# Modulation products of layer 0 in pairs of row blocks, layer 1's partition sums in one piece

## The chip, the cores and the metric

One core of a Trainium2 chip runs the kernel. The metric is device microseconds of one execution, the median over several runs. A profiled execution of the same kernel, whose rows are shown below, has its own time.

## The reference, cut to what matters

A trunk of two layers works on 128 context tokens and 256 latent tokens of 1024 features. Each layer takes a conditioning vector (one for context, one for latent tokens), makes six modulation vectors of it with a 1024 x 6144 matrix, and uses them around a mixer and a feed-forward block:

```
def trunk_layer(x, cvec, lp, init, latent):
    mod = jax.nn.silu(cvec.astype(jnp.float32)) @ lp['w_mod'] + lp['b_mod']
    sh1, sc1, g1, sh2, sc2, g2 = jnp.split(mod[:, None, :], 6, axis=-1)
    h = rmsnorm(x, lp['norm_mix_pre']) * (1.0 + sc1) + sh1
    mix, states = mixer(h, lp, init, latent)      # retention | Hyena long convolution | mLSTM
    x1 = x + g1 * rmsnorm(mix, lp['norm_mix_post'])
    h = rmsnorm(x1, lp['norm_ffn_pre']) * (1.0 + sc2) + sh2
    out = x1 + g2 * rmsnorm(conv_ffn(h, lp), lp['norm_ffn_post'])
```

The change concerns the first line alone: the product of two vectors (context and latent) with `w_mod`, 25 MB a layer.

## The kernel before

The large projections (`w_in`, `w_out`, `w_up`, `w_down`) run on TensorE with weights split into a high and a low part: a raw chunk is loaded (`raw`, line 333, issued by SyncE, called SP), ScalarE casts it (`hi`, L278), VectorE subtracts (`lo`, L255), and three products are made for each block (activations `hh`, `hl` by weights `hi`, `lo`). Every matmul is recorded at line 208 (`mm`), every transpose at L212 (`tp`); `b` is a PSUM bank.

The modulation matrix of a layer is cut in three superblocks of 2048 columns (s = 0, 1, 2) and eight row blocks of 128 rows, 1 MB each (`mraw`, two buffers). A row block by the two conditioning columns (`sil`) is a narrow product: 4 products of 512 columns whose outputs lie at partitions 0, 32, 64 and 96 of one bank. These are the narrow products of this text; all others, which fill the array, are called wide. Superblock 0 of layer 0 is made at the start. Superblocks 1 and 2 of layer 0 (`mod`) are streamed beside the projections of the mixer: they are two generators in a queue, and `fill`, called once for each chunk of weights of the mixer's projections (`weights`), takes one step of it. A step loads one row block and issues its four products. After the eighth, `mod_finish` loads a bias tile (`modbm`, in a buffer of the same two), adds it on VectorE, writes gates to DRAM (`gd`), and transposes the result on TensorE.

For layer 1 (`mod_beside`) the products are made on VectorE during layer 0's feed-forward block: two accumulators `macc` (one for each conditioning vector, r = 0 and 1) of 2048 columns take each row block times one column of `sil`, in pieces of 512 columns. At the end eight products with `onesel` (a column of ones that picks one output row) sum over partitions on TensorE into one bank, for each of the three superblocks.

Each engine works its instructions off in order. That order comes from a list scheduler that goes by priorities and by its own estimate of times, except where the code fixes it (`issue_after`: behind a given instruction on its engine; `high_priority`: earlier in the list). SP issues the loads in its own order too, and a load whose buffer isn't free yet holds back those behind it.

Of the kernel before, what the change touches and what calls it, by code (L numbers as in the profile page):

```python
# [37 lines left out]
# the largest float32 by which half a turn stays within the range of the sine  # L38
# [3 lines left out]
# ---------------------------------------------------------------- host side: layout and shape constants  # L42
# [8 lines left out]
def _constants():  # L51
# [6 lines left out]
    # minus one for each of the three parts of a head's row  # L58
# [10 lines left out]
    # even and odd tokens, the lower half of the frequencies: the upper half is their sum with  # L69
    # the other sign, conjugated  # L70
# [31 lines left out]
def _layout(inp):  # L102
# [8 lines left out]
    # rows of the modulation vectors: block j of 512 columns sits at partitions 32j (context) and 32j + 1 (latent)  # L111
# [14 lines left out]
    def token_major(m):  # L126
        # (L, D, 4*384) -> per group of 384 columns, two chunks of four 128-row blocks
        m = m.reshape(L, 2, 4, 128, 4, 384)
        return m.transpose(0, 4, 1, 3, 2, 5).reshape(L, 8, 128, 1536)
# [3 lines left out]
    # the gates ride along with the first 384 columns  # L133
# [7 lines left out]
    # per-partition columns  # L141
# [11 lines left out]
    # the filter networks of both layers side by side, 64 partitions each  # L153
# [34 lines left out]
# ---------------------------------------------------------------- device side  # L188

class Trunk:  # L190
    # banks of the accumulators of w_out, by block of tokens
# [13 lines left out]
    # -------- small helpers  # L205
# [8 lines left out]
    def in_order(self, engine):  # L214
        """The engines in self.strict take their work as it is written here."""
        last = getattr(self, engine)
        return self.tc.issue_after(last.ins) if engine in self.strict and last else nullcontext()

    def after(self, *last):
        """Behind these on their engines."""  # L220
        stack = ExitStack()
        for i in last:
            stack.enter_context(self.tc.issue_after(i.ins))
        return stack

    # -------- PSUM: eight banks, each a queue of its own
# [3 lines left out]
    def turn(self, s):  # L230
        """The next bank of a set taken in turns."""
# [54 lines left out]
    def rms(self, s2):  # L286
        """The reciprocal root of the mean square, from the two halves of the mean."""
# [6 lines left out]
    def log_sigmoid(self, out, z, P, n):  # L294
        """min(z, 0) - log1p(exp(-|z|)), log1p with the rounding of its argument put back."""
# [11 lines left out]
    # -------- weights  # L307
# [18 lines left out]
    def load_weights(self):  # L326
        """The loads of the next chunk of the stream, in halves."""
# [14 lines left out]
    def splits(self, key, raws):  # L342
        """High and low parts of a chunk, in steps."""
        halves, steps = [], []
        # at the turn of a block the buffers are still taken, but the one of the spectra is idle
# [5 lines left out]
        for raw in raws:  # L351
            m = raw.shape[1]
            hi, lo = new("hi"), new("lo")
            # finer where the vector engine also has the norms between two projections to do
# [22 lines left out]
    # -------- setup  # L377
    def setup(self):
# [21 lines left out]
        # silu of both conditioning vectors, as stationary columns  # L400
# [15 lines left out]
    def start(self, fp):  # L416
        """Modulation and normalised rows of the first projection, and the filter spectra of both
        layers beside them; the loads in the order in which they are needed."""
# [7 lines left out]
        def rows(k):  # L426
            """Modulation weights, in the buffers of the weights as long as these are idle."""
# [44 lines left out]
        def warm(n):  # L472
            """Products of no use that take the tensor engine's clock out of its rest while the first
            loads are on their way."""
            for _ in range(n):
                self.mm(spin, idle[:, :128], idle)
# [16 lines left out]
        # the bias  # L493
# [69 lines left out]
    def fill(self, n=1):  # L563
        """Streams the next blocks of modulation weights beside the projections."""
# [11 lines left out]
    def mod(self, l, s):  # L576
        """Superblock s of the modulation of layer l: (sh1 | sc1), (g1 | sh2), (sc2 | g2)."""
        nc = self.nc
        ps = self.md()
        for k in range(KD):  # L580
            raw = self.wraw.tile([128, 2048], F32, tag="mraw", name=self.nm("mraw"), bufs=2)
            nc.sync.dma_start(raw, self.I["w_mod"][l, 128 * k:128 * k + 128, 2048 * s:2048 * s + 2048])
            for j in range(4):
                self.mm(ps[32 * j:32 * j + 32, :], self.sil[:, k, :], raw[:, 512 * j:512 * j + 512], k == 0, k == KD - 1)
            if k < KD - 1:
                yield False
        self.mod_finish(l, s, ps, self.md)

    def mod_beside(self, l, s):
        """The same with the products on the vector engine, where only that one has time to spare."""  # L590
# [18 lines left out]
        for j in range(4):  # L609
            for r in range(2):  # L610
                self.mm(ps[32 * j:32 * j + 32, :], self.onesel[:, r, :], acc[r][:, 512 * j:512 * j + 512], r == 0, r == 1)
# [33 lines left out]
    def gate_rows(self, l, g):  # L645
        """A gate times its norm gain, over all partitions: [128, context / latent, D]."""
# [5 lines left out]
    # -------- hyena filter spectra  # L652
    def filter_hidden(self, fp, w1, w2, col, meanwhile):
        """The hidden layers of the filter networks of both layers: [128, tokens] for each layer,
        64 rows of its own and a row of ones."""
# [4 lines left out]
        for i, wt in enumerate((w1, w2)):  # L660
# [5 lines left out]
            # in turns, less the nearest whole number  # L666
# [15 lines left out]
    def filter_taps(self, fp, l, h, w3):  # L682
        """Sum and difference of the forward and the backward filters."""
# [15 lines left out]
    def filter_spectra(self, fp, l, taps):  # L699
        nc = self.nc  # L700
        # spectra [frequency, tile, cos / sin, order, channel]
# [15 lines left out]
    def butterfly(self, s, d, a, b):  # L717
        """s = a + b, d = a - b, of two PSUM tiles."""
# [8 lines left out]
    # -------- normalised, modulated activations, transposed and split  # L727
# [4 lines left out]
    def norm_pre(self, t):  # L732
        """A diagonal of the reciprocal root mean squares of the rows of x."""
# [9 lines left out]
    def norm_T(self, t, where, h, psf):  # L743
        """Tokens of block t modulated, transposed and split into the tiles of h."""
# [31 lines left out]
    def norm_T_after(self, *a):  # L776
        """norm_T behind the products queued so far."""
# [6 lines left out]
    def group(self, key, l, g, between=None):  # L784
        """Token-major columns g of an input projection: three [128, 384] accumulators."""
# [12 lines left out]
        if key == "m" and g == 0:  # L798
            # the first tokens are there before the last ones
# [36 lines left out]
    def heads_T(self, src, tag):  # L836
        """[128 tokens, 4 * 96] -> [96, 4, 128]."""
# [7 lines left out]
    def head_norm(self, src, out):  # L845
        """out = src * 0.5 * rsqrt(mean(src^2) + eps) by head, [128, 4, 96]; src in SBUF."""
# [9 lines left out]
    # -------- gates of the mLSTM  # L856
    def gates(self, l, pss):
# [5 lines left out]
        # [token, direction, tile, head]  # L863
# [6 lines left out]
        # the splits of the next weights let the gates go first  # L870
# [3 lines left out]
    def stabilisers(self, l, g5, lf):  # L874
# [9 lines left out]
        # rows [head, direction, tile, token]  # L884
# [13 lines left out]
        # [head, (previous, last), direction, tile]  # L898
# [21 lines left out]
        # previous and last stabilisers over all partitions: [128, 2, direction, tile, head]  # L920
# [22 lines left out]
    def row_parts(self, mr):  # L943
        """The stabilisers as three bfloat16 parts that add up to them, 32 partitions apart."""
# [13 lines left out]
    # -------- mLSTM  # L958
# [117 lines left out]
    def channel_major(self, outs, ws, hh, hl):  # L1076
        """Two [128 columns, 384 tokens] products from a chunk [rows of k, 2 * 128 columns]."""
# [9 lines left out]
    # -------- Hyena  # L1087
    def long_conv(self, z, o):
        """z: two [128 channels, 384] tiles -> PSUM tiles of the long convolution, the latent rows
        with the even ones first."""  # L1090
# [473 lines left out]
```

## Time and profile before

| | |
|---|---|
| median of 3 runs | 1358.76 us (1355.83 to 1360.96) |
| span of the profiled execution | 1355.0 us |
| what lies between the median and that span | 3.8 us |
| TensorE busy in the span | 1339.3 us, 99% |
| VectorE busy | 890.6 us, 66% |
| ScalarE busy | 568.8 us, 42% |
| DMA moved | 217.27 MB, mean 160 GB/s |

The span runs from the first to the last instruction of the profiled execution, and sums are made against it. Ends of matmuls are modelled in the profile, so durations of neighbours overlap a little, and the distance of two starts is the safer measure of what an instruction costs. Layer 0's streamed modulation lies between 60 and 222 us of the span, layer 1's sums at 437, 539 and 645 us.

### The profile page before, as it was taken

To read this page: it belongs to the slowest core of one execution; us is meant where nothing else is said; L and a number is where in the kernel's file an instruction comes from. 1 tells how busy PE (TensorE), PEld (TensorE's weight loads), DVE (VectorE), ACT (ScalarE), POOL (GpSimd) and SP (SyncE) were. 2 spreads that over 40 slices of the span, in tenths; PEclk is the share of its full clock that TensorE was granted. 3 is DMA by queue.
4 is the path that set the end of the run, shared out by engine and by line. 5 is a ranking of instruction groups with operands and counts; after the bars stand their busy time and mean duration, and the time that the engine had idled before them with its cause. 6 is when DMAs were issued, how large, how long until landed. Compare 5 with 4: busy or idle time off the path is not lost.

```text
span 1355.0 us, 19419 instructions
## 1 busy us (share of the span) xinstructions
PE 1339.3 (99%) x7527; PEld 1206.1 (89%) x7527; DVE 890.6 (66%) x1594; ACT 568.8 (42%) x944; POOL 35.3 (3%) x64
## 2 busy tenths in 40 slices
PE   8999999999999999999999999999999999999997
PEld 2788788889998998899899999988999999999996
DVE  5657666667887899799557578666645545545445
ACT  3654253464333333333247543546433333333333
POOL 1100000000000000000000000000000000000000
PEclk9999999999999999999999999999999999999999
DMA  9864557344665565665335232424434334333331
GB/s 354 290 249 148 181 168 238 101 164 151 212 227 172 191 237 176 212 221 181 116 112 192 95 95 73 143 92 173 143 118 137 126 117 136 124 121 131 124 122 50
DMA packets 59101, 217.27 MB, mean 160 GB/s; under 512 B 7214, under 2 KB 9456, under 8 KB 53632
## 3 DMA queue, kind: packets, MB, share of 16 engines
q1 hardware_dynamic: 59008, 216.02, 46.7%
q8 instruction: 59, 0.97, 0.3%
q14 instruction: 34, 0.28, 0.1%
HBM read 210.06 MB, written 5.94 MB: 159 GB/s over the span
## 4 chain that ended last, share of the span: by engine, by line
PE 91%; DMA 5%; DVE 2%; ACT 1%; issue 1%; POOL 0%; SPq 0%; DVEq 0%; POOLq 0%; ACTq 0%
PE b L208 90%; DMA mraw<-in_w_mod 1%; DMA raw<-in_w_up 1%; PE b L212 1%; DMA hi<-in_w_mod 1%; DMA lo<-in_w_mod 1%; DMA raw<-in_w_in_m 1%; DVE lo L255 1%; ACT junk L274 0%; ACT hi L278 0%; DMA c_tri<-in_c_tri 0%; DMA w<-in_f_w 0%; DVE mr L908 0%; POOL rr L291 0%; DVE x L266 0%
## 5 line engine op out<-in xcount | busy, mean ns | idle before, releaser
L255 DVE TENSOR_TENSOR lo<-raw,hi 128x1024 fp32r<-128x1024 f32 (+3 forms) x288 | 321.2, 1129 | 216.9 <-ACT hi L278 214.3
L278 ACT CAST hi<-raw 128x1024 fp32r<-128x1024 f32 (+3 forms) x288 | 275.4, 973 | 411.7 <-PE b L208 387.5
L208 PE MATMUL b<-hh,lo 128*128 128x384 f32 (+1 forms) x1120 | 367.9, 336 | 0.0
L208 PE MATMUL b<-hh,hi 128*128 128x384 f32 (+2 forms) x1120 | 364.8, 334 | 0.0
L208 PE MATMUL b<-hl,hi 128*128 128x384 f32 x1088 | 362.5, 338 | 0.0
L208 PEld LDWEIGHTS b<-hh,hi 128*128 128x128 f32 x1120 | 205.7, 188 | 4.6 <-issue 2.5
L208 PEld LDWEIGHTS b<-hh,lo 128*128 128x128 f32 x1120 | 208.0, 188 | 0.1
L208 PEld LDWEIGHTS b<-hl,hi 128*128 128x128 f32 x1088 | 203.7, 188 | 1.2
L208 PE MATMUL b<-lo,hh 128*128 128x384 f32 (+2 forms) x474 | 164.8, 352 | 1.9 <-DVE lo L255 1.9
L208 PE MATMUL b<-hi,hh 128*128 128x384 f32 (+2 forms) x468 | 165.5, 357 | 0.9 <-ACT hh L1347 0.8
L208 PE MATMUL b<-hi,hl 128*128 128x384 f32 (+2 forms) x468 | 162.7, 351 | 0.0
L266 DVE SCALAR_TENSOR_TENSOR cv<-b,pcol,cv 128x127 f32<-128x127 f32 (+1 forms) x256 | 100.6, 414 | 93.9 <-ACT cv L274 89.4
L208 PE MATMUL b<-lo,gh 128*128 128x512 f32 x384 | 151.7, 395 | 0.0
L208 PE MATMUL b<-hi,gh 128*128 128x512 f32 x384 | 150.6, 392 | 0.0
L208 PE MATMUL b<-hi,gl 128*128 128x512 f32 x384 | 150.2, 391 | 0.0
L274 ACT ACTIVATE cv<-b,pcol 128x384 f32<-128x384 f32 x64 | 43.0, 672 | 178.6 <-PE b L208 178.4
L266 DVE SCALAR_TENSOR_TENSOR macc<-mraw,sil,macc 128x512 f32<-128x512 f32 x168 | 113.3, 746 | 0.0
L208 PEld LDWEIGHTS b<-hi,hh 128*128 128x128 f32 x468 | 87.8, 188 | 16.1 <-issue 8.0
L208 PEld LDWEIGHTS b<-lo,hh 128*128 128x128 f32 x474 | 89.1, 188 | 7.3 <-DVE lo L255 3.7
L208 PEld LDWEIGHTS b<-hi,hl 128*128 128x128 f32 x468 | 87.9, 188 | 4.5 <-issue 0.7
L208 PEld LDWEIGHTS b<-hi,gh 128*128 128x128 f32 x384 | 72.1, 188 | 17.5 <-issue 2.5
L208 PEld LDWEIGHTS b<-lo,gh 128*128 128x128 f32 x384 | 72.1, 188 | 17.2 <-issue 3.4
(242 smaller groups left out, 1221.2 us busy)
## 6 DMA issues: line engine op xcount, KB each, us to landing
raw<-in_w_up SPq DMA_DIRECT2D x128, 512.0 KB, 4.6
mraw<-in_w_mod SPq DMA_DIRECT2D x40, 1024.0 KB, 5.1
raw<-in_w_down SPq DMA_DIRECT2D x64, 512.0 KB, 4.3
raw<-in_w_in_r SPq DMA_DIRECT2D x32, 384.0 KB, 3.1
raw<-in_w_in_m SPq DMA_DIRECT2D x24, 384.0 KB, 6.3
raw<-in_w_out SPq DMA_DIRECT2D x16, 512.0 KB, 4.1
raw<-in_w_in_h SPq DMA_DIRECT2D x12, 512.0 KB, 3.7
mraw<-in_w_mod SPq DMA_DIRECT2D x8, 512.0 KB, 10.0
```

The lines of the kernel that those rows point to most:

```text
L208: self.pe = self.nc.tensor.matmul(out, lhsT=lhsT, rhs=rhs, start=start, stop=stop, **kw)
L212: self.pe = self.nc.tensor.transpose(out, in_, self.ident[:n, :n])
L255: self.dve = self.nc.vector.tensor_tensor(o, a, b, op)
L266: self.dve = self.nc.vector.scalar_tensor_tensor(o, a, s, b, op0, op1)
L274: self.scalar = self.nc.scalar.activation(o, a, f, **kw)
L278: self.scalar = self.nc.scalar.copy(o, a)
```

## The change

`mod` takes two row blocks in a step: it loads both, then issues eight products, those of the second block first, so that a superblock has four steps instead of eight and the whole stream of layer 0 is taken by 7 calls of `fill` instead of 15. A new function `narrow` issues such a list so that each product stands right behind the one before it on TensorE. `mod_beside` issues its eight sums by `narrow` too, those of r = 1 ahead of those of r = 0, and within each the column groups in the order 3, 0, 1, 2. Comments and docstrings were dropped, which moves line numbers and nothing else.

```diff
     def mod(self, l, s):
         ps = self.md()
-        for k in range(KD):
-            raw = self.wraw.tile([128, 2048], F32, tag="mraw", name=self.nm("mraw"), bufs=2)
-            nc.sync.dma_start(raw, self.I["w_mod"][l, 128 * k:128 * k + 128, 2048 * s:2048 * s + 2048])
-            for j in range(4):
-                self.mm(ps[32 * j:32 * j + 32, :], self.sil[:, k, :], raw[:, 512 * j:512 * j + 512], k == 0, k == KD - 1)
-            if k < KD - 1:
+        for k in range(0, KD, 2):
+            raws = []
+            for kk in (k, k + 1):
+                raw = self.wraw.tile([128, 2048], F32, tag="mraw", name=self.nm("mraw"), bufs=2)
+                self.nc.sync.dma_start(raw, self.I["w_mod"][l, 128 * kk:128 * kk + 128, 2048 * s:2048 * s + 2048])
+                raws.append((kk, raw))
+
+            self.narrow([
+                (ps[32 * j:32 * j + 32, :], self.sil[:, kk, :], raw[:, 512 * j:512 * j + 512], kk == k + 1 == 1, kk == k == KD - 2)
+                for kk, raw in raws[::-1] for j in range(4)])
+            if k < KD - 2:
                 yield False
         self.mod_finish(l, s, ps, self.md)
 
+    def narrow(self, products):
+
+        with ExitStack() as stack:
+            for p in products:
+                self.mm(*p)
+                stack.enter_context(self.tc.high_priority(offset=300))
+                stack.enter_context(self.tc.issue_after(self.pe.ins))
+
     def mod_beside(self, l, s):
...
         ps = self.bank(6)
-        for j in range(4):
-            for r in range(2):
-                self.mm(ps[32 * j:32 * j + 32, :], self.onesel[:, r, :], acc[r][:, 512 * j:512 * j + 512], r == 0, r == 1)
+
+        self.narrow([
+            (ps[32 * j:32 * j + 32, :], self.onesel[:, r, :], acc[r][:, 512 * j:512 * j + 512], r == 1, r == 0)
+            for r in (1, 0) for j in (3, 0, 1, 2)])
         self.mod_finish(l, s, ps, lambda: self.bank(7))
```

The first place is TensorE in layer 0, one of the cut row blocks of before, beside the inverse transform of the long convolution (`c_inv_p`; `zt` is its input, `c_fwd` the forward transform):

```order
L208 MATMUL b_313_1487<-zt_1476,c_fwd_p 128x256 x2
L208 MATMUL b_314_1488<-zt_1476,c_fwd_s 128x256 x2
L208 MATMUL b_315_1489<-zt_1476,c_fwd_s 128x256 x2
L208 MATMUL b_345_1580<-mraw_1581,sil 32x512
L208 MATMUL b_329_1526<-c_inv_p,y_1505 128x128 x2
L208 MATMUL b_330_1533<-c_inv_p,y_1505 128x128 x2
L208 MATMUL b_345_1580<-mraw_1581,sil 32x512 x3
```

After, the last pair of the stream stands ahead of the convolution, between wide products:

```order
L208 MATMUL b_306_1442<-hh_374,hi_1376 128x384
L208 MATMUL b_306_1442<-hl_375,hi_1376 128x384
L208 MATMUL b_205_971<-mraw_1457,sil 32x512 x4
L208 MATMUL b_205_971<-mraw_1455,sil 32x512 x4
L208 MATMUL b_306_1442<-hh_374,lo_1377 128x384
```

The block that was cut is whole now and has its partner with it; the forward and inverse transforms of the convolution have nothing between them but wide products.

The second place is SP, which issues the loads, around the last row blocks of superblock 1 and the bias tile of before:

```order
L333 DMA raw_1721<-in_w_in_r 128x768 [waits DMAHW6_49,DVE_49]
L619 DMA modbm_1566<-in_mod_bm 128x1024 [waits DMAHW7_49,DMAHW0_49,PE_49]
L333 DMA raw_1723<-in_w_in_r 128x768 [waits DVE_49]
L333 DMA raw_1802<-in_w_in_r 128x768 [waits DMAHW4_49,DMAHW1_49,DVE_49]
L333 DMA raw_1804<-in_w_in_r 128x768 [waits DMAHW5_49,DMAHW2_49,DVE_49]
L582 DMA mraw_1581<-in_w_mod 128x2048 [waits DMAHW3_49,PE_49]
L630 DMA gd_76<-modbm_1566 2x512 [waits DVE_49]
```

After, at the end of superblock 2:

```order
L583 DMA mraw_1455<-in_w_mod 128x2048 [waits DMAHW4_49,PE_49]
L583 DMA mraw_1457<-in_w_mod 128x2048 [waits DMAHW3_49,PE_49]
L333 DMA raw_1777<-in_w_in_r 128x768 [waits DMAHW1_49,DVE_49]
L333 DMA raw_1779<-in_w_in_r 128x768 [waits DMAHW2_49,DVE_49]
L632 DMA modbm_1467<-in_mod_bm 128x1024 [waits DMAHW0_49,PE_49]
L607 DMA mraw_3224<-in_w_mod 128x2048 [waits DMAHW7_49,PE_49]
```

Each of the two loads of a pair now waits for TensorE's products of the pair before it (the wait for PE), and so does the bias tile; the raw weights stand behind the two loads.

The third place is TensorE in layer 1's second group of sums, before (`gh` and `gl` are the activations of the feed-forward block):

```order
L208 MATMUL b_947_5090<-macc_4216,onesel 32x512
L208 MATMUL b_947_5090<-macc_4217,onesel 32x512
L208 MATMUL b_947_5090<-macc_4216,onesel 32x512
L208 MATMUL b_947_5090<-macc_4217,onesel 32x512
L208 MATMUL b_947_5090<-macc_4216,onesel 32x512
L208 MATMUL b_649_3143<-hi_4993,gh_4759 128x512
L208 MATMUL b_947_5090<-macc_4217,onesel 32x512
L208 MATMUL b_947_5090<-macc_4216,onesel 32x512
L208 MATMUL b_649_3143<-lo_4994,gh_4759 128x512
L208 MATMUL b_649_3143<-hi_4993,gl_4760 128x512
L208 MATMUL b_649_3143<-hi_4995,gh_4840 128x512
L208 MATMUL b_947_5090<-macc_4217,onesel 32x512
```

and after, where the products into `b_649` and `b_650` all come first:

```order
L208 MATMUL b_650_3144<-hi_4995,gh_4840 128x512
L208 MATMUL b_650_3144<-lo_4996,gh_4840 128x512
L208 MATMUL b_650_3144<-hi_4995,gl_4841 128x512
L208 MATMUL b_947_5090<-macc_4217,onesel 32x512 x4
L208 MATMUL b_947_5090<-macc_4216,onesel 32x512 x4
L208 MATMUL b_651_3145<-hi_4993,gh_4759 128x512
```

Twelve wide products, six into each of the two banks, moved ahead of the sums, and the eight sums stand together.

## Rows read from the trace of the kernel before

**Rows 1.** The page: busy time and share of the span of each engine

```profile
PE 1339.3 (99%) x7527; PEld 1206.1 (89%) x7527; DVE 890.6 (66%) x1594; ACT 568.8 (42%) x944; POOL 35.3 (3%) x64
```

**Rows 2.** The page: the chain that ended last, by engine

```profile
PE 91%; DMA 5%; DVE 2%; ACT 1%; issue 1%; POOL 0%; SPq 0%; DVEq 0%; POOLq 0%; ACTq 0%
```

**Rows 3.** Windows: length, busy PE, PEld, DVE, ACT, POOL; clock, DMA share, GB/s

```profile
60.00:147.00 87.00, 86.54 (x591) 74.51 (x590) 54.16 (x142) 43.73 (x84) 3.04 (x3) 1.00 0.59 202
...
60.00:70.00 10.00, 10.00 (x63) 8.30 (x62) 6.12 (x18) 7.53 (x12) 0.00 (x0) 1.00 0.93 344
```

**Rows 4.** TensorE's timeline, 62 to 71: start, duration, instructions merged

```profile
62.11 0.35 PE L208 MATMUL b<-hi,hl 128*128 128x400 f32 x1
62.39 1.92 PE L208 MATMUL b<-mraw,sil 128*32 128x512 f32 x16
64.24 0.44 PE L208 MATMUL b<-hi,hh 128*128 128x384 f32 x1
64.53 0.33 PE L208 MATMUL b<-lo,hh 128*128 128x384 f32 x1
...
70.42 0.34 PE L208 MATMUL b<-hi,hl 128*128 128x384 f32 x1
```

**Rows 5.** TensorE's timeline, a whole row block at 91

```profile
91.17 1.06 PE L208 MATMUL b<-mraw,sil 128*32 128x512 f32 x8
92.17 0.45 PE L208 MATMUL b<-hi,hh 128*128 128x384 f32 x1
```

**Rows 6.** TensorE's timeline, a cut row block at 161 to 165

```profile
161.27 1.04 PE L208 MATMUL b<-mraw,sil 128*32 128x512 f32 x2
...
164.23 1.06 PE L208 MATMUL b<-mraw,sil 128*32 128x512 f32 x6
```

**Rows 7.** TensorE's timeline, two waits: in brackets the idle time and its releaser

```profile
152.32 1.02 PE L208 MATMUL b<-mraw,sil 128*32 128x512 f32 x2 [0.60 <-DMA mraw<-in_w_mod]
...
76.40 0.42 PE L208 MATMUL b<-bd,ones 4*128 4x48 f32 x2 [0.44 <-DVE bd L255]
```

**Rows 8.** TensorE's timeline, layer 1's first group of sums

```profile
434.28 0.39 PE L208 MATMUL b<-hi,gh 128*128 128x512 f32 x1
...
436.81 0.39 PE L208 MATMUL b<-hi,gl 128*128 128x512 f32 x1
437.13 1.94 PE L208 MATMUL b<-macc,onesel 128*32 128x512 f32 x16
439.00 0.51 PE L208 MATMUL b<-hi,gh 128*128 128x512 f32 x1
```

**Rows 9.** TensorE's timeline, layer 1's second group of sums

```profile
539.36 2.58 PE L208 MATMUL b<-macc,onesel 128*32 128x512 f32 x10
541.88 0.49 PE L208 MATMUL b<-hi,gh 128*128 128x512 f32 x1
542.30 1.05 PE L208 MATMUL b<-macc,onesel 128*32 128x512 f32 x4
...
544.17 1.04 PE L208 MATMUL b<-macc,onesel 128*32 128x512 f32 x2
```

**Rows 10.** VectorE's timeline, the last products of that group

```profile
539.24 2.73 DVE L266 SCALAR_TENSOR_TENSOR macc<-mraw,sil,macc 128x512 f32<-128x512 f32 x4
```

**Rows 11.** Issues of row blocks (L582, 60 to 150) and bias tiles (L619)

```profile
L582 SPq DMA_DIRECT2D mraw<-in_w_mod x7: 327/357/462, 63.5 to 145.2; - x7
...
DMA to landing us min/median/max: 4.8/5.0/5.2
...
DMA to landing us min/median/max: 3.5/3.8/4.1
```

**Rows 12.** VectorE's timeline around the bias tile of superblock 1

```profile
142.71 1.23 DVE L255 TENSOR_TENSOR lo<-raw,hi 128x1024 fp32r<-128x1024 f32 x1 [0.85 <-PE b L212]
...
145.21 0.69 DVE L255 TENSOR_TENSOR modbm<-b,modbm 128x512 f32<-128x512 f32 x1 [1.01 <-PE b L208]
...
146.46 0.48 DVE L266 SCALAR_TENSOR_TENSOR modbm<-modbm,c_onecol 128x256 f32<-128x256 f32 x1
```

**Rows 13.** The page's DMA issues: count, KB each, us to landing

```profile
mraw<-in_w_mod SPq DMA_DIRECT2D x8, 512.0 KB, 10.0
```

More of the change, by code (lines that the diff above doesn't have):

```diff
@@ L576, in mod @@
     def mod(self, l, s):
-        nc = self.nc
         ps = self.md()
-        for k in range(KD):
-            raw = self.wraw.tile([128, 2048], F32, tag="mraw", name=self.nm("mraw"), bufs=2)
-            nc.sync.dma_start(raw, self.I["w_mod"][l, 128 * k:128 * k + 128, 2048 * s:2048 * s + 2048])
-            for j in range(4):
-                self.mm(ps[32 * j:32 * j + 32, :], self.sil[:, k, :], raw[:, 512 * j:512 * j + 512], k == 0, k == KD - 1)
-            if k < KD - 1:
+        for k in range(0, KD, 2):
[8 more added lines that the diff above has]
+            if k < KD - 2:
                 yield False
         self.mod_finish(l, s, ps, self.md)
+    def narrow(self, products):
[4 more added lines that the diff above has]
+                stack.enter_context(self.tc.issue_after(self.pe.ins))
     def mod_beside(self, l, s):
```

## Prediction

> **What bounds the kernel now.** I read the page first. TensorE is busy in 99% of the span, VectorE in 66% [rows 1], and 91% of the chain that ended last is TensorE's [rows 2]. The stretch that layer 0's modulation shares has 86.54 us of TensorE work in 87.00 us, at a granted clock of 1.00 (the 2.4 GHz level), with the DMA engines at 0.59 [rows 3]. So a microsecond that TensorE saves is a microsecond of the time, and one that it waits is lost; VectorE, ScalarE and DMA count only where TensorE waits for them. All working below is therefore about what TensorE starts when.
>
> Next I went to TensorE's timeline for the price of its ordinary work. From 64.53 to 70.42 it starts 34 wide products (384 columns), 0.173 us apart [rows 4].
>
> Then the narrow products, 32 output columns each, which lie four beside one another in the array. The timeline merges those that follow without a wide one between; each product leaves two records. Three forms occur in layer 0:
> - a whole row block (four products, x8): 91.17 to 92.17, 1.00 us [rows 5]. Nine of the sixteen blocks look so;
> - a block that other products cut in two: x2 has a duration of 1.04 us and x6 one of 1.06 [rows 6], each as much as the whole block's 1.06, of which the next product's start cuts off 0.06. So I count 0.98 and 1.00. Five blocks look so;
> - two blocks that happen to stand together (x16): 62.39 to 64.24, 1.85 us [rows 4]. This is once.
>
> At each border there is a gap beyond the ordinary pitch: 62.11 to 62.39 is 0.28 and 64.24 to 64.53 is 0.29 [rows 4], where 0.17 to 0.18 is usual. That makes 0.22 us for each separate group. What the reader should see: the price goes by groups, not by products. Two products cost what four cost, and a pair of blocks costs 1.85 against 2.00 + 0.22 for two singles.
>
> **The change, layer 0.** The same 64 products remain; they stand as eight pairs. Before: 1 pair x (1.85 + 0.22) + 9 singles x (1.00 + 0.22) + 5 cut blocks x (0.98 + 1.00 + 0.44) = 2.07 + 10.98 + 12.10 = 25.1 us. After: 8 x 2.07 = 16.6. **Gain 8.5 us**, all of it on the path. Two waits should go as well: 0.60 us at 152.32 for a row block that is late (the stream ends earlier now), and 0.44 at 76.40 for VectorE (a pair now stands ahead of it) [rows 7]. **Gain 1.0.**
>
> **The change, layer 1.** Here the sums over partitions stand beside VectorE's last products. The first group is already whole: x16 in 1.87 us from 437.13 to 439.00 [rows 8], so nothing is to be had. It also shows that two products on the same output columns, one right behind the other, cost no more than others do. The second group is cut in three: x10 2.52 (539.36 to 541.88), x4 0.99 and x2 0.98 (durations 1.05 and 1.04 less the 0.06) [rows 9], with 3 x 0.22 5.15 us, against 1.87 + 0.22 = 2.09: 3.06. The third group has the same three pieces (644.59, 647.54 and 649.42 in the timeline, lengths alike to 0.01). **Gain 6.1 us.** Why x10 took 2.52: VectorE's last four columns run from 539.24 to 541.97 [rows 10], and the sums follow them. After the change the eight products wait for the last column at once. The order puts twelve more 512-column products ahead. Eleven steps from 434.28 to 436.81 are 2.53 us, 0.23 each [rows 8], so twelve are 2.76, so TensorE comes there at 539.36 + 2.76 = 542.1, after 541.97. The wait is near zero by a margin of 0.1; had I misjudged by two products it would cost 0.5 for each group, which the range holds.
>
> **The change, the loads.** This is what must be paid. Two buffers hold the row blocks. Before, one block was loaded while the other was used. Now both are taken by a pair, and the next two loads can go only when the pair's last product is done. One load lands after 5.0 us (4.8 to 5.2) [rows 11]; the second has to move another 1.05 MB, and the stretch 60 to 70 moved 344 GB/s at 0.93 busy [rows 3], 370 GB/s if full: 2.8 us. A pair is therefore there 0.2 + 5.0 + 2.8 = 8.0 us after the last one ended. Until then TensorE has 41 to 46 products between two pairs. I estimate these covers from the order at the prices above as 8.1, 8.2, 8.5 and 7.6 us for pairs 4, 6, 7 and 8, and 8.6, 9.1 and 9.9 for pairs 2, 3 and 5 (transposes and small products at the prices of their rows). Six cover it barely or well, one lacks 0.4; for scatter in landing I take **1.0 us** in all.
>
> A rule speaks against this price. The Trainium skill, "DMA: Bandwidth & Descriptors", section "Where 436 GB/s comes from", says that from HBM the memory side binds at about 358 GB/s for a core. By that rule the second megabyte would take 2.9 us instead of 2.8 (an estimate from that page), and the sum would be worse by under a microsecond over the seven pairs. The stretch at 344 GB/s agrees with it.
>
> More than the rate, what matters is what else is in the queue. In 60 to 147 the core moves 202 GB/s x 87 us = 17.6 MB with seven row blocks among it [rows 3, 11]; after, fourteen. That is 24.9 MB, 286 GB/s, 77% of 370. It fits, but with little room where the weights' own loads are bunched, since all of them wait in SP's order. Where they queue behind a wait for a row block's buffer, the weights come up to 8 us later; they were loaded 10 to 40 us ahead, so I cost that at nothing. If this slack were gone, TensorE would wait by the missing part for each chunk.
>
> The second cost is the bias tile of `mod_finish`, which lives in the same two buffers. Before, it was there long before its use at 145.21: what VectorE waited for there was TensorE, not a DMA [rows 12]. Now it can be issued only when the last pair has been used. It lands 3.8 us later [rows 11]. VectorE stands in order: the add, a subtraction of the weights between them (1.23), and two products, 0.69 + 1.23 + 0.96 in all [rows 12]. Then come the transposes on TensorE, which waited for nothing before. So they are ready 0.2 + 3.8 + 2.9 = 6.9 us after the pair. TensorE has about 5.0 us of work in between (13 wide products, 2.25; nine transposes, 1.0; ten wide products, 1.75). That is a wait of 2 us, and as the short convolution stands behind the add on VectorE, the transposes of its rows are late by another half: **2.5 us** for superblock 2. For superblock 1 there are 24 wide products and more to cover it: nothing. The inverse transforms of the convolution lose the narrow products that filled a gap: **0.5 us**. Bounds of all the new waits: 0 if everything lands as the fastest row does and VectorE is ahead, 10 and more if loads land late (below). I take 1.0 + 2.5 + 0.5 = 4.0.
>
> **Sum.** -8.5 - 1.0 - 6.1 + 4.0 = -11.6. The profiled execution's span was 1355.0, which gives 1343.4. The median of the runs shown, 1358.76, lies 3.8 above that span, so the forecast is 1343.4 + 3.8 = 1347.2, or 1347. That is 0.85% less than before. About 0.5%, 6.8 us, can be told from no change here.
>
> **The rivals.**
> - No new waits show: the loads land at 7.5 or less and the bias tile is covered. Then -15.6 with up to 1.5 of it lost, about 1344. For it: landings in this stage scatter little, 4.8 to 5.2 [rows 11]. Against: the bias tile's wait comes out of a plain sum of rows.
> - The pairs land late, and layer 0's gain is eaten: within 0.5%. With landing L after the issue, each pair waits L + 0.2 less its cover. At L = 10, the four tight ones wait 8.4 together (40.8 - 32.4) and the three loose ones 3.0 (30.6 - 27.6); with 3.0 for the bias tile and the transforms that makes 14.4, net -1.2, 1357.6. For it: where the queue was full, loads of half the size took 10.0 [rows 13], and all of SP's loads are in one queue. Against: the 5.0 of single blocks in this very stage. This case runs from L = 9.1 (waits of 8.8) up.
> - Slower: the same mechanism further on. From L = 11.2 the waits are 7 x 11.4 - 60.0 + 3.0 = 22.8, net +7.2, and the kernel is slower by over 0.5%. At L = 12 it is 28.4, net +12.8, 1371.6. It needs more than twice the landing that the rows of the stage show for one block, with only a second block added. Little speaks for it.
> - The groups don't stay whole, or don't run at the price of rows 4. The order shows every pair and sum in one piece. If the pairs cost two singles less one border, 2.22, the gain shrinks by 1.2; this is inside the range.
>
> **How the numbers follow.** Forecast 0.58, no waits 0.19, late pairs 0.18, slower 0.05. The forecast's own range is 1343.5 to 1351.5 (new waits 0.5 to 8). Over all, 1341 to 1356: below, the case without waits, 1355.0 - 15.6 + 3.8 = 1343.2, less 2 for the scatter of a median (the three runs lie 5 us apart); above, late pairs up to about L = 9.7. Chances: faster by over 0.5% 0.77, within 0.5% 0.18, slower 0.05.
>
> **What the profile after would show.** Right: eight x16 groups on `mraw,sil` between 60 and 150 (one of them may lie a little ahead), each near 1.85 to the next wide product; no such products after 150; three x16 groups on `macc,onesel` of about 1.9; a wait of TensorE for `modbm` or `hy` of about 2.5 near 150; waits for `mraw` of under 1 us each. Wrong: waits for `mraw` of 1 to 3 us ahead of most pairs (the loads are late), a wait of VectorE's sums at the second and third group of layer 1, or waits for `raw`, `hi` or `lo` past 150 (weights late behind SP's order). The forecast fails most easily at the landing of two blocks at once, which no row of before shows.

## The result, and the profile after

The changed kernel takes 1344.22 us (median of 4 runs, 1343.04 to 1347.23), where the kernel before, run beside it, took 1357.3 (4 runs, 1355.21 to 1360.96). The ratio is 0.9897, with a 95% interval of 0.988 to 0.9913. It was faster, by 13 us; the forecast was 1347.

The profiled execution has a span of 1341.3 us, 13.7 less than the 1355.0 of before. The page's first section and its chain of waits, which answer to [rows 1, 2]:

```profile
span 1341.3 us, 19422 instructions
...
PE 1326.4 (99%) x7527; PEld 1205.8 (90%) x7527; DVE 890.5 (66%) x1594; ACT 569.1 (42%) x944; POOL 35.2 (3%) x64
...
PE 90%; DMA 5%; DVE 2%; ACT 2%; issue 1%; POOL 0%; SPq 0%; DVEq 0%; POOLq 0%; ACTq 0%
```

TensorE has the same 7527 instructions and is busy 12.9 us less; every other engine does what it did. So it is the price of TensorE's own work that fell, and hardly its waits.

**Where it came from.** I cut the span at two marks that both kernels have: the start of the first pair (62.39 before, 62.78 after) and the start of layer 1's first sums (437.13 and 430.08). Between them lies all of layer 0's stream: 374.74 us before and 367.30 after, 7.44 less. Behind the second mark lie 917.86 us before and 911.18 after, 6.68 less. The start is 0.39 later. 7.44 + 6.68 - 0.39 = 13.7. The first of the two is the sharper: a second profile of the changed kernel has 367.99 between the marks, and 914.25 behind the second. Busy time of TensorE between the marks (columns as in [rows 3]), before and after:

```profile
62.39:437.13 374.74, 372.12 (x2238) 331.76 (x2237) 265.22 (x512) 165.21 (x290) 9.39 (x12) 1.00 0.54 185
62.78:430.08 367.30, 364.52 (x2237) 331.90 (x2236) 265.71 (x512) 165.20 (x290) 9.38 (x12) 1.00 0.55 189
```

TensorE is busy 7.60 us less there, and idle 2.78 instead of 2.62.

TensorE's timeline shows the groups as planned. A first pair and its borders, and layer 1's second and third group, which answer to [rows 4, 9]:

```profile
62.50 0.35 PE L208 MATMUL b<-hi,hl 128*128 128x400 f32 x1
62.78 1.92 PE L208 MATMUL b<-mraw,sil 128*32 128x512 f32 x16
64.63 0.44 PE L208 MATMUL b<-hi,hh 128*128 128x384 f32 x1
64.92 0.33 PE L208 MATMUL b<-lo,hh 128*128 128x384 f32 x1
...
534.94 1.92 PE L208 MATMUL b<-macc,onesel 128*32 128x512 f32 x16
536.79 0.50 PE L208 MATMUL b<-hi,gh 128*128 128x512 f32 x1
...
637.44 1.92 PE L208 MATMUL b<-macc,onesel 128*32 128x512 f32 x16
639.29 0.50 PE L208 MATMUL b<-hi,gh 128*128 128x512 f32 x1
```

A pair costs 1.85 us to the next start, as the accidental pair of before did, and each group of sums costs 1.85 where the three pieces had 4.49. VectorE's last four columns of the second group:

```profile
532.06 2.73 DVE L266 SCALAR_TENSOR_TENSOR macc<-mraw,sil,macc 128x512 f32<-128x512 f32 x4
```

They end at 532.06 + 2.73 = 534.79, 0.15 ahead of the sums at 534.94. There is no wait, and the prediction had 0.1 of margin.

I summed all groups with their borders (start to the next start, and what the steps into and out of the group exceed 0.173 us, or 0.23 beside the 512-column products; a step between two groups is counted once, and waits are left out). Layer 0: 20.67 + 3.24 = 23.91 us in 20 groups before, 14.91 + 1.26 = 16.17 in 8 groups after. Layer 1: 10.82 + 1.41 = 12.23 in 7 groups, and 5.56 + 0.62 = 6.18 in 3.

**The waits.** TensorE's waits between the two marks, after; in brackets the idle time and what ended it. They answer to [rows 7]:

```profile
76.80 0.42 PE L208 MATMUL b<-bd,ones 4*128 4x48 f32 x2 [0.16 <-DVE bd L255]
...
136.91 1.92 PE L208 MATMUL b<-mraw,sil 128*32 128x512 f32 x16 [0.79 <-DMA mraw<-in_w_mod]
```

Besides these there are 0.21 at 119.4 and 0.09 at 152.8; what stands from 247 us on (0.42, 0.77, 0.17, 0.16) was there before too. Only the seventh pair waits for its loads. SP's timeline shows when loads were issued (x2 are the two of a pair, with their duration together). The last two lines answer to [rows 11]. They hold only the loads whose landing the trace tells, three of the sixteen row blocks (L583) and one bias tile, that of superblock 1 (L632):

```profile
138.04 1.19 SPq L583 DMA_DIRECT2D mraw<-in_w_mod  x2
...
147.49 0.33 SPq L632 DMA_DIRECT2D modbm<-in_mod_bm  x1
...
DMA to landing us min/median/max: 6.4/6.7/7.1
...
DMA to landing us min/median/max: 4.4/4.4/4.4
```

The seventh pair's products start at 136.91 and end near 138.77. The next loads go at 138.04, which is halfway (136.91 + 0.93) and 0.2, not at the end. One of the two buffers is free as soon as the four products of its block are done, and the load that comes next takes that one. The bias tile does the same: the eighth pair starts at 146.36, and the tile is issued at 147.49, 0.7 ahead of the pair's end at 148.21.

### The profile page after: what moved, and what is told of

The parts are those of the page before. It is cut to its first block, busy times and chain, and to the rows that moved or that the text cites. A ratio compares the mean times of both kernels' runs of the same rounds, so it can differ in the third digit from the quotient of the medians.

```text
span 1341.3 us, 19422 instructions
## 1 busy us (share of the span) xinstructions
PE 1326.4 (99%) x7527; PEld 1205.8 (90%) x7527; DVE 890.5 (66%) x1594; ACT 569.1 (42%) x944; POOL 35.2 (3%) x64
## 4 chain that ended last, share of the span: by engine, by line
PE 90%; DMA 5%; DVE 2%; ACT 2%; issue 1%; POOL 0%; SPq 0%; DVEq 0%; POOLq 0%; ACTq 0%
PE b L208 89%; DMA mraw<-in_w_mod 1%; PE b L212 1%; DMA raw<-in_w_up 1%; DMA hi<-in_w_mod 1%; DMA lo<-in_w_mod 1%; DMA raw<-in_w_in_m 1%; ACT hi L278 1%; DVE lo L255 1%; ACT junk L274 0%; DMA c_tri<-in_c_tri 0%; DVE mr L921 0%; DMA w<-in_f_w 0%; POOL rr L291 0%; DVE x L266 0%
## 5 line engine op out<-in xcount | busy, mean ns | idle before, releaser
L208 PEld LDWEIGHTS b<-hi,gl 128*128 128x128 f32 x384 | 72.1, 188 | 15.6
```

The lines of the kernel that those rows point to most:

```text
L208: self.pe = self.nc.tensor.matmul(out, lhsT=lhsT, rhs=rhs, start=start, stop=stop, **kw)
```

## Experiments

All compare with the kernel before, run on the same chip beside them. "The stretch" is the time between the two marks above in a profiled execution: 374.74 us before, 367.30 after. It has the layer 0 part alone, and is far sharper than the medians, whose intervals are some 2 us wide on either side.

**Each part alone.** One kernel has the new sums and `mod` of the kernel before, the other the pairs and the sums of the kernel before:

```diff
-        self.narrow([
-            (ps[32 * j:32 * j + 32, :], self.onesel[:, r, :], acc[r][:, 512 * j:512 * j + 512], r == 1, r == 0)
-            for r in (1, 0) for j in (3, 0, 1, 2)])
+        for j in range(4):
+            for r in range(2):
+                self.mm(ps[32 * j:32 * j + 32, :], self.onesel[:, r, :], acc[r][:, 512 * j:512 * j + 512], r == 0, r == 1)
```

> Only layer 1's sums stand together, layer 0's row blocks are streamed one at a time as before. Theory (the price goes by groups and their borders; the two parts add up): the second and third group of sums fall from 4.5 us in three pieces to 1.85 in one, with two borders less each, so 6.1 to 6.5 us less than the kernel before, about 1351, ratio 0.9954. Rival (the pieces only filled time in which TensorE would have waited for VectorE's last columns): a wait for the accumulators appears ahead of both groups, and the gain is under 3 us.

> Only layer 0's row blocks go in pairs, layer 1's sums are as before. Theory: 7.0 to 7.7 us less than the kernel before, about 1350, ratio 0.9945, with one wait for a pair of about 0.8 us, as in the changed kernel. Rival (the parts help one another, so that the gain of one needs the other): the two parts alone add up to clearly less than the 13 us of both.

Sums alone: 1351.1 us, ratio 0.9954 (0.9939 to 0.9968), stretch 375.29. Pairs alone: 1350.34, ratio 0.9946 (0.993 to 0.9961), stretch 367.73. The second group of sums in either:

```profile
543.38 1.93 PE L208 MATMUL b<-macc,onesel 128*32 128x512 f32 x16
545.23 0.50 PE L208 MATMUL b<-hi,gh 128*128 128x512 f32 x1
```

```profile
533.29 2.58 PE L208 MATMUL b<-macc,onesel 128*32 128x512 f32 x10
535.80 0.49 PE L208 MATMUL b<-hi,gh 128*128 128x512 f32 x1
536.23 1.05 PE L208 MATMUL b<-macc,onesel 128*32 128x512 f32 x4
...
538.10 1.04 PE L208 MATMUL b<-macc,onesel 128*32 128x512 f32 x2
```

The first fence is the kernel with new sums, the second the one with the old. No wait appears ahead of the whole group. The parts save 0.46% and 0.54%, together 1.0%; both at once save 1.0% too (0.9897; 0.9911 in the second run below). Each rival falls.

The stretch of the first kernel serves as a second measure of the layer 0 of before, which it has unchanged. Its granted clock was 0.95 in 70 to 80 us and 0.88 in 80 to 90. From the first narrow group to the third it takes 30.35 us (63.12 to 93.47), where the kernel before takes 28.78 (62.39 to 91.17), so 1.57 of the 375.29 go to that, which leaves 373.7, 1.0 less than the 374.74. The wait of 0.60 for a row block [rows 7] isn't there either:

```profile
153.94 1.05 PE L208 MATMUL b<-mraw,sil 128*32 128x512 f32 x2
```

Its load, issued at 147.50, was there within 6.4 us, where before it took 7.1 (145.20 to 152.32). So that wait comes and goes without the change.

**Whole row blocks, no pairs.** This tells the two halves of the layer 0 part apart: that no block is cut, and that two stand together.

```diff
-        for k in range(0, KD, 2):
-            raws = []
-            for kk in (k, k + 1):
...
+        for k in range(KD):
+            raw = self.wraw.tile([128, 2048], F32, tag="mraw", name=self.nm("mraw"), bufs=2)
...
+            self.narrow([
+                (ps[32 * j:32 * j + 32, :], self.sil[:, k, :], raw[:, 512 * j:512 * j + 512], k == 0, k == KD - 1)
+                for j in range(4)])
```

> As the changed kernel, but layer 0 takes one row block in a step, its four products glued together so that no block is cut; the sums of layer 1 are those of the change. Theory (a group costs about 1.0 us up to four products and 0.85 for four more, with 0.2 for its borders): one pair at 2.07 and fourteen singles at 1.22 are 19.2 us against 16.3 for eight pairs, so layer 0 gains 4.9 of the 7.7 from whole blocks alone, and the kernel is 2 to 3 us slower than the changed one, less the 0.8 of the pair's wait: 1346 to 1347. Rival (it is the pairing that gains, the cuts cost little): 1350 or more.

> The kernel with single whole row blocks once more, for a second profile of its stretch, beside the changed kernel's of 367.3 and 368.0. Theory (whole groups are nearly all of it, the pairing adds under 1 us): 367.5 to 368.3 us again. Rival (the pairing is worth 2 us, and the first profile hid it by chance): 369 to 370.

First run: 1344.92 us, ratio 0.9911 (0.9895 to 0.9927), stretch 367.88. Second: 1347.27, ratio 0.9932 (0.9917 to 0.9947), stretch 369.37, but there the granted clock was 0.97 in 70 to 80 us and 0.86 in 80 to 90, where the first run had 1.00 (the 2.4 GHz level); TensorE had been busy for 10.00 us of each of the slices 50 to 60 and 60 to 70, and for 9.54 of 70 to 80, just as in the first run. From the first narrow group to the third it takes 30.35 us, against 28.78 in the first run, 1.57 more, which leaves 367.8; uncorrected it would be the rival's number. Groups in the stretch: 15 with 18.16 us, no wait for a row block. Busy time between the marks in the first run, and a block that was cut before:

```profile
61.56:429.44 367.88, 366.16 (x2238) 330.91 (x2237) 265.03 (x512) 165.22 (x290) 9.38 (x12) 1.00 0.56 188
...
156.17 0.34 PE L208 MATMUL b<-hh,lo 128*128 128x384 f32 x1
156.44 1.07 PE L208 MATMUL b<-mraw,sil 128*32 128x512 f32 x8
157.43 1.27 PE L208 MATMUL b<-c_inv_s,g 128*128 128x128 f32 x9
```

This kernel differs from the one before in layer 0 by nothing but the five cuts, and its groups cost 23.91 - 18.16 = 5.75 us less. TensorE is busy 372.12 - 366.16 = 5.96 less: 1.2 for each cut. The stretch is 6.9 shorter than before, but 0.9 of that are waits, the 0.60 above all, which the sums alone didn't have either. Four profiles of pairs with the same order in the stretch (the changed kernel twice, the pairs alone, and the last column's kernel below) have 367.30, 367.99, 367.73 and 367.01. So the pairing as such adds about 0.4 us to what whole blocks give, although TensorE is busy 366.16 - 364.52 = 1.64 less with it: most of the rest goes for the wait of the seventh pair (0.79, 1.19, 0.91 and 0.94 in those four) and smaller ones. The theory held, and more strongly than it was put: I had expected the pairing to be worth 1 to 2 us net.

**Pairs with the first block first.** The products follow the order of the loads:

```diff
-                (ps[32 * j:32 * j + 32, :], self.sil[:, kk, :], raw[:, 512 * j:512 * j + 512], kk == k + 1 == 1, kk == k == KD - 2)
-                for kk, raw in raws[::-1] for j in range(4)])
+                (ps[32 * j:32 * j + 32, :], self.sil[:, kk, :], raw[:, 512 * j:512 * j + 512], kk == 0, kk == KD - 1)
+                for kk, raw in raws for j in range(4)])
```

> As the changed kernel, but within a pair the products of the block that is loaded first come first. In the order of instructions five of the eight pairs then fall apart into singles, one of these cut again. Theory (price by groups): three pairs at 2.07, nine singles at 1.22 and one cut block at 2.4 are 19.6 us against 16.3, so 3 us slower than the changed kernel, less any wait saved because the first block's buffer is used and freed earlier: 1346 to 1348. Rival (the order within a pair matters through the loads alone): the buffers come free earlier, and it is as fast as the changed kernel or faster, 1344 or less.

1344.01 us, ratio 0.9902 (0.9886 to 0.9919). There are 14 groups with 18.03 us in the stretch, 1.9 more than with whole pairs, and waits of 0.31 and 0.35 for row blocks in place of one of 0.79. The stretch is 371.12; the granted clock was 0.99 and 0.84 in 70 to 90, also behind busy slices. That I put at 0.01 x 10 + 0.16 x 10 = 1.7 us, an estimate, which leaves 369.4. That is 1.9 above the mean of the four, less than the 3 expected. The median is the rival's number, though, and doesn't tell this kernel from the changed one. The rows bear out the price by groups; by the time the experiment is inconclusive. What the reversed order does is seen in the groups: when the first product waits for the block that lands last, all eight can go at once, and nothing gets between.

**Pairs not tied together.** In `mod` the products are issued as a plain list:

```diff
-            self.narrow([
+            for p in [
...
-                for kk, raw in raws[::-1] for j in range(4)])
+                for kk, raw in raws[::-1] for j in range(4)]:
+                self.mm(*p)
```

> As the changed kernel, but the products of a pair aren't tied to one another on TensorE: the order then cuts two of the eight pairs, one in two pieces (5 and 3 products), one in three (1, 5 and 2 blocks' pieces of 1, 4 and 3). Theory (a cut costs a whole group's price and two borders): 1.2 us for the first and about 2 for the second, so 3 us more in the stretch of layer 0 than the changed kernel's 367.3: 370. Rival (cuts are filled by work that would wait otherwise): under 1 us more.

1345.5 us, ratio 0.9929 (0.9911 to 0.9947), stretch 370.25, which is 2.95 more than the changed kernel's profile. One of the cut pairs:

```profile
126.15 1.05 PE L208 MATMUL b<-mraw,sil 128*32 128x512 f32 x2
127.13 1.13 PE L208 MATMUL b<-cn,qT 96*128 96x97 f32 x8
128.19 1.06 PE L208 MATMUL b<-mraw,sil 128*32 128x512 f32 x8
129.19 1.13 PE L208 MATMUL b<-v,w 128*128 128x97 f32 x8
130.25 1.06 PE L208 MATMUL b<-mraw,sil 128*32 128x512 f32 x6
131.24 0.45 PE L208 MATMUL b<-hi,hl 128*128 128x384 f32 x1
```

Pieces of one, four and three products all cost 1.0 us (each product leaves two records). The middle one takes three products of one block and one of the other, all at different partitions: what counts is that the four places are different, not the block. 

The changed kernel itself ran beside this one and the two that follow:

> The changed kernel itself, beside the three that follow. 1343 to 1345 us, ratio to the kernel before 0.990; in the stretch from the first pair to layer 1's first sums 367.3 us within 0.3 where the granted clock is 1.00.

The changed kernel again: 1343.23 us (6 runs), ratio 0.9911 (0.9895 to 0.9928), stretch 367.99. That is 0.7 above its first profile and outside what I had expected; 0.4 of it is the seventh pair's wait, 1.19 instead of 0.79.

**The last column first, accumulators in turns.** In layer 1's sums:

```diff
-            for r in (1, 0) for j in (3, 0, 1, 2)])
+            for j in (3, 0, 1, 2) for r in (1, 0)])
```

> As the changed kernel, but in layer 1's sums the two accumulators take turns on each group of columns, with the columns that VectorE finishes last still first. Theory (it is enough that the first product of the group is the one that VectorE finishes last; two products on the same columns one behind the other cost nothing more): three groups of x16 at 1.87 instead of 1.85, the same time as the changed kernel. Rival (products on the same columns wait for one another): each group takes 3 us or more, 3 to 6 us in all.

1344.93 us, ratio 0.9921 (0.9903 to 0.9939). The second group is whole and costs 1.88:

```profile
534.69 1.95 PE L208 MATMUL b<-macc,onesel 128*32 128x512 f32 x16
536.57 0.50 PE L208 MATMUL b<-hi,gh 128*128 128x512 f32 x1
```

All three groups with borders are 6.25 us, against 6.18. Whether the two accumulators take turns, so that products on the same columns follow one another, is of next to no account (0.03 us a group here). The first product is still the one that VectorE finishes last, and the sums stay whole. Whether that order or `narrow` keeps them whole was not tried apart in layer 1.

**Both buffers free at the end.** In `mod` the two blocks take turns:

```diff
-                for kk, raw in raws[::-1] for j in range(4)])
+                for j in range(4) for kk, raw in raws[::-1]])
```

> As the changed kernel, but within a pair the products of the two blocks take turns, so that both buffers are free only at the pair's end, not one of them halfway. Theory (the halfway release is why the pairs' loads are nearly hidden, where the prediction let both go at the end): each pair of loads, and the bias tile, starts 0.9 us later; the one wait for a pair grows from 0.8 to about 1.7, and one or two others of up to 1 us appear, 1 to 3 us in all over the changed kernel's stretch of 367.3. Rival (the loads have room enough wherever they start): the same stretch within 0.5 us.

1344.83 us, ratio 0.9921 (0.9905 to 0.9938), stretch 366.56: not longer. The loads do go at the pair's end: the seventh pair stands from 139.34 to 141.21, and the next two are issued at 141.36. The bias tile of superblock 1 is now waited for, which it wasn't:

```profile
107.41 0.44 PE L212 MATMUL b<-c_ident,modbm 128*128 128x128 f32 x2 [0.73 <-DVE modbm L266]
...
141.36 0.80 SPq L583 DMA_DIRECT2D mraw<-in_w_mod  x2
```

But the pairs wait only 0.18, 0.11 and 0.08. Up to 160 us all waits come to 1.25 here and in the changed kernel alike; that the stretch is 0.7 shorter lies in a wait for `lo` near 269 us, 0.77 there, as before the change, and 0.1 here. The later release also moved the order: the last three pairs start 11.4, 10.2 and 10.4 us after the one before, where the changed kernel has 10.7, 10.9 and 9.4. So the theory that the halfway release hid the loads fell as it was stated; with another order there is room enough for the loads without it. With the order held, it wasn't tried.

**One load less in the queue.** In the changed kernel SP issues the table `rel` (124.8 us), a weight chunk (125.2) and the seventh pair's loads (127.1 on) close together. The table's load is left out in layer 0:

```diff
-        nc.sync.dma_start(rel, self.I["c_rel"])
+        if l:
+            nc.sync.dma_start(rel, self.I["c_rel"])
+        else:
+            nc.gpsimd.memset(rel, 0.5)
```

> As the changed kernel, but the table of distances that retention loads in layer 0 (256 KB, issued at 124.8 us, 2.3 us ahead of the seventh pair's loads) is filled with a constant on GpSimd instead of loaded, so retention's decays in layer 0 are not the reference's. Theory (the one wait for a pair, 0.79 to 1.19 us in four profiles, is that this load and a weight chunk share the DMA engines with the pair): 256 KB at 370 GB/s are 0.7 us, so the wait falls to 0.1 to 0.5 and the stretch by as much. Rival (it is the distance of the two pairs on TensorE that is too short): the wait stays at 0.8 to 1.2.

1345.95 us, ratio 0.9915 (0.9899 to 0.9932), stretch 368.14. The seventh pair's wait is 0.15, as the theory had it. But the pair then ends earlier, and the eighth one waits:

```profile
136.70 1.92 PE L208 MATMUL b<-mraw,sil 128*32 128x512 f32 x16 [0.15 <-DMA mraw<-in_w_mod]
...
147.08 1.92 PE L208 MATMUL b<-mraw,sil 128*32 128x512 f32 x16 [0.93 <-DMA mraw<-in_w_mod]
```

A wait of 0.35 for the bias tile comes with it. So the wait was moved, not removed: the load took part in it, but the stretch gained nothing. Which of the loads in the queue makes the eighth pair late was not tried.

## Why the prediction came out as it did

**The price by groups: right.** Layer 0's groups were put at 25.1 and 16.6 us, and measured 23.91 and 16.17. The gain of 8.5 became 7.7 (7.60 by TensorE's busy time). A border between 384-column products is 0.20 (0.27 in and 0.28 out, less 0.173 each), near the 0.22 of [rows 4]. Beside transposes and other small products the steps are mostly 0.15 to 0.21, so that all 20 borders of before come to 3.24, 0.16 each. Part of that lies in the count, since a transpose's own step is 0.11 and not 0.173; the busy time needs no such count. One reading was off without harm: the x2 and x6 of [rows 6] are one product and three, so what the rows show is that one product costs what four cost, not that two do.

The Trainium skill, "TensorEngine Tiling (Array Packing)", section "Key Properties", says that a change of the tiling mode drains TensorE. By that each group would pay at its two ends whatever its length, and the traces agree as far as that goes: 0.27 and 0.28 beside a pair (62.50 to 62.78, 64.63 to 64.92), 0.27 ahead of a single block (156.17 to 156.44). That the drain is the cause they don't show. A 384-column product behind a transpose, without a change to narrow products, takes 0.26 to the next start as well (152.93 to 153.19 in the lines below); only the step into a group is long by itself, for into a transpose it is 0.18 (153.37 to 153.55).

**What earns the gain: not separated in the prediction.** It added the cuts and the pairing up in one term. With single whole blocks TensorE is busy 5.96 us less, out of the 7.60 of the change; the pairing brings the other 1.64 and gives most of it back in waits.

**Layer 1: right.** 6.1 forecast, 6.05 measured (12.23 to 6.18). VectorE's last column came 0.15 ahead of the sums.

**The waits that go: right in size, in part by chance.** 0.60 is gone, and 0.44 became 0.16; 0.9 against 1.0. But the 0.60 was missing with the sums alone too, where layer 0 streams as before, so the change need not be what removed it.

**The waits that come: wrong, and this is what the forecast was off by.** Put at 4.0, they were 0.79 + 0.21 + 0.09 = 1.1. Two steps failed:
- "the next two loads can go only when the pair's last product is done". One goes halfway, 0.9 earlier. The price of the pairs' waits, 1.0, was nonetheless about right (0.79), but on another pair, the seventh instead of the eighth. The covers came out as estimated, 8.3 for 8.5 at the seventh (127.83 to 136.12, where its wait begins) and 7.6 for 7.6 at the eighth (138.77 to 146.36). The loads scattered about the 8.0 us worked out: the third pair's second load, issued at 76.69, landed 6.4 later, the eighth pair was there within 7.6 us of the end of the seventh, and the seventh only 9.1 after the end of the sixth. One load ahead of it in the queue took part in that, as the last experiment shows.
- "now it can be issued only when the last pair has been used", of the bias tile. It was issued 0.7 us ahead of the pair's end. VectorE did wait for it, as this row and the two behind it show, and TensorE's transposes came after it without a wait of their own:

```profile
151.17 0.69 DVE L255 TENSOR_TENSOR modbm<-b,modbm 128x512 f32<-128x512 f32 x1 [1.20 <-DMA modbm<-in_mod_bm]
151.78 1.21 DVE L255 TENSOR_TENSOR lo<-raw,hi 128x1024 fp32r<-128x1024 f32 x1
152.91 0.87 DVE L266 SCALAR_TENSOR_TENSOR modbm<-modbm,c_onecol 128x256 f32<-128x256 f32 x2
```

```profile
152.79 0.38 PE L212 MATMUL b<-c_ident,hy 128*128 128x128 f32 x1
152.93 0.42 PE L208 MATMUL b<-hh,lo 128*128 128x384 f32 x1
153.19 0.34 PE L208 MATMUL b<-hh,hi 128*128 128x384 f32 x1
153.37 0.34 PE L208 MATMUL b<-hl,hi 128*128 128x384 f32 x1
153.55 0.38 PE L212 MATMUL b<-c_ident,modbm 128*128 128x128 f32 x2
```

From the pair's end at 148.21 to the transposes is 5.34 us, and TensorE was busy in all but 0.09 of them. What was put at 6.9 against a cover of 5.0 was 5.3 against 5.3: 0.9 from the earlier issue, 0.1 from the load (3.7 from its issue to the add), 0.5 because the first transposes need only the first half of the last products, and the cover was sized 0.25 too small. So 2.5 us became 0.09.

The third price, 0.5 us for the inverse transforms, did not appear at all.

**The rate of the loads.** The prediction weighed a rule of the Trainium skill, "DMA: Bandwidth & Descriptors", section "Where 436 GB/s comes from", by which the memory side binds at about 358 GB/s. In 40 slices of 60 to 150 us after, the last line giving GB/s:

```profile
GB/s 246 399 234 437 422 412 385 132 426 414 310 147 117 411 420 385 173 279 368 360 219 300 324 4 0 113 408 411 7 149 235 359 411 288 197 265 430 402 197 200
```

Slices of 2.25 us reach 437 and three in a row lie above 410. The measurement decides: 358 did not bind here, and the 370 that I had worked out was low as well. The mean came out as forecast, 289 GB/s in 60 to 147 us against the 286 of the text.

**The sum by its measured terms:** -7.7 - 0.9 + 1.1 in layer 0 is -7.5 (7.44 by the marks), -6.05 in layer 1, together -13.6, against the -11.6 forecast and 13.7 between the spans. This is nearest to the rival without new waits, 1344, which was given 0.19; the forecast's own range holds it near its lower end because the gains were sized right.

## What to carry to other kernels

Products that fill a quarter of the array are priced by the group in which they stand on TensorE, not one by one: up to four at different places cost as one, and a group pays for its borders. Look in the timeline for such groups that were cut, and tie them together. Let the product whose operand is ready last be the first: in layer 0 groups fell apart here without the tie, and with it when the order was reversed. Before a buffer is costed as "free at the end", find which product reads it last: the load that waits for it may go well before the group is over.

## What the runs showed of the hardware that was not expected

- One 128x512 product into 32 columns, four into the four quarters, and three of one block with one of another all take 0.98 to 1.00 us to the next start; eight take 1.85. A single cut costs 1.2 us, as much as a whole further row block.
- Taking one 256 KB load out of the queue removed 0.6 to 1.0 us of wait at one pair and brought 0.9 at the next.
- Executions differ in short dips of the granted clock, two of the same program (the single blocks) among them: 0.84 to 0.88 in the slice 80 to 90 us of three, 0.90 to 0.93 in the first 20 us of three. The first kind cost 1.57 us by the starts of the same instructions in each of two. The second kind shows no cost: those three reach the first pair at 61.6 to 61.8 us, the other nine at 62.4 to 63.4. At differences under 2 us a stretch between two marks, with its clock beside it, told more than the medians.
